# The opening of an encoder block: low weight parts behind the row statistics on GpSimd, rows five to seven taken together, one group's first sums later

## The chip, the cores and the metric

The kernel runs on one core of a Trainium2 chip. A core has five engines with queues of their own: TensorE (PE in the profile, with its weight loads as PEld), VectorE (DVE), ScalarE (ACT), GpSimd (POOL) and SyncE (SP, which here only issues transfers). Each works off its instructions in the order of the program; between engines they wait for one another by semaphores. The metric is the device time of one execution in microseconds (us).

## The reference

One transformer-like layer over 1024 tokens of width 1024, in float32. A layer norm of the input feeds one large projection with 11776 columns; dilated attention, a bidirectional gated recurrence, a merge, two more layer norms and a SwiGLU follow.

```python
h = layer_norm(x, ln_in_g, ln_in_b)
for l in range(DEPTH):                       # DEPTH = 1
    proj = h @ w_in[l]                       # (1024 x 1024) @ (1024 x 11776)
    aq, ak, av, hq, hf_fwd, hf_bwd, hi, hg, ga, gh = jnp.split(proj, split_idx, axis=-1)
    att = dilated_attention(aq, ak, av, slopes)
    rec = hgrn2(hq, hf_fwd, hf_bwd, hi, hg, lower_bounds[:, l], hgrn_norm_g[l])
    merged = jax.nn.sigmoid(ga) * (att @ w_att_up[l]) + jax.nn.sigmoid(gh) * (rec @ w_hgrn_up[l])
    h = layer_norm(DEEPNORM_ALPHA * h + merged @ w_o[l], ln1_g[l], ln1_b[l])
    gate, up = jnp.split(h @ w_ffn_in[l], 2, axis=-1)
    h = layer_norm(DEEPNORM_ALPHA * h + (jax.nn.silu(gate) * up) @ w_ffn_out[l], ln2_g[l], ln2_b[l])
```

Only the first layer norm and the first columns of `h @ w_in` are touched by the change.

## The kernel before

**Numbers in two parts.** TensorE multiplies in a rounded float32 format. A float32 operand is split into a high part (a rounding copy) and a low part (the difference), and each product is three matmuls: high by high (line 272), high by low (line 273) and low by high (line 274). For a weight block of 128x512 the high part is a cast on ScalarE (`w_hi`, line 214) and the low part a subtraction on GpSimd (`w_lo`, line 224), both in `split`. For the activations the high part is written by ScalarE (line 326) and the low part by VectorE (lines 401 and 402).

**The large product.** `h @ w_in` goes by a seven-product scheme over 2x2 blocks of 512. For each set of columns the products are numbered 1, 2, 6, 5, 7, 3, 4. Product 1 takes weight block `a11` with the activation form `b11`, product 2 `a12` with `b21`, product 6 the sum `s2` with `t2`, product 5 `s1` with `t1`, product 7 `s3` with `t3`, product 3 `s4` with `b22`, product 4 `a22` with `t4`. `stream` issues them in a list: first product 1 of two column sets for two groups each (places 0 to 3), then product 2 of the same four (places 4 to 7), then product 6 of the first set (places 8 and 9, one for each group), and so on. `prep(i)` splits the weights of place i; `sums(i)` makes `s1` (line 694, VectorE), `s2` (line 695, VectorE) and `s3` (line 696, GpSimd) for a product 6.

**The opening.** `phase0` makes the activation forms while `stream` already runs. The tokens come as eight row tiles of 128x1024, called row 0 to row 7 here. For each row `stats(tt)` gives mean and variance (two `bn_stats` on VectorE, line 343, an aggregate, line 345) and then three tiny GpSimd instructions (lines 346 to 348: add epsilon, power of minus one half, the shift); `norm(tt, q)` scales half q of the row on ScalarE (line 326) or VectorE (line 353); `turn` transposes it into PSUM on TensorE (line 362). Rows 0 to 3 give `b11` (half 0) and `b21` (half 1), rows 4 to 7 give the other column half of both, from which `t1`, `t2`, `b22`, `t3` and `t4` are made by subtractions (line 391 and others). The pool of row tiles has seven buffers, so row 7 is loaded only when row 0 has been transposed.

**What sets the order.** The kernel is recorded under a scheduler that reorders each engine's instructions by its own estimates of time. `ordered` and `behind` add an order without a semaphore: while `strict` is true, ScalarE's and VectorE's instructions of the opening stand in the order written; afterwards the scheduler may interleave them. `behind(ins, last)` puts one instruction behind another. `self.later` holds calls of `sums` for places 8 and 9 back until `phase0` has reached a given point.

Of the kernel before, what the change touches and what calls it, by code (L numbers as in the profile page):

```python
# [14 lines left out]
OP = mybir.AluOpType  # L15
# [64 lines left out]
class Block:  # L80
# [115 lines left out]
    def stats(self, pool, y, tag):  # L196

        nc = self.nc
        st = self.tiny.tile([128, 2, 6], F32, name=f"bn{tag}", tag="bnst", bufs=3)
        for j in range(2):  # L200
            nc.vector.bn_stats(st[:, j, :], y[:, HALF * j:HALF * (j + 1)])
        mv = self.tiny.tile([128, 4], F32, name=f"mv{tag}", tag="bnmv", bufs=3)
        self.rstd(mv, st)
        return mv
# [103 lines left out]
    def phase0(self, pool, work):  # L308


        nc, xs, banks = self.nc, [], {}
# [6 lines left out]
        w21 = [self.half("v21") for _ in range(4)]  # L318

        strict = True  # L320
        WARM = (11, 7, 6, 4)
        self.turned_last = None
        nbin = self.spare[:, 0:4]
# [5 lines left out]
        def dve(ins):  # L329
            return self.ordered("xdve", ins) if strict else ins  # L330
# [9 lines left out]
        def stats(tt):  # L340
            st = self.tiny.tile([128, 2, 6], F32, name="bn0", tag="bnst", bufs=3)
            for j in range(2):
                dve(nc.vector.bn_stats(st[:, j, :], xs[tt][:, HALF * j:HALF * (j + 1)]))
            mv = self.mv0[:, tt, :]
            dve(nc.vector.bn_aggr(mv[:, 0:2], st))
            nc.gpsimd.tensor_scalar(mv[:, 2:3], mv[:, 1:2], LN_EPS, None, op0=OP.add)
            nc.gpsimd.tensor_tensor(mv[:, 2:3], mv[:, 2:3], self.mhalf[:, 0:1], OP.pow)
            nc.gpsimd.tensor_scalar(mv[:, 3:4], mv[:, 0:1], mv[:, 2:3], -1.0, op0=OP.mult, op1=OP.mult)

        def norm(tt, q):  # L350
            x, mv = xs[tt][:, HALF * q:HALF * (q + 1)], self.mv0[:, tt, :]
            if tt > 5 and q == 0 or 0 < tt < 4 and q:
                return dve(nc.vector.tensor_scalar(x, x, mv[:, 2:3], mv[:, 3:4], op0=OP.mult, op1=OP.add))
            return act(x, x, AF.Identity, bias=mv[:, 3:4], scale=mv[:, 2:3])
# [49 lines left out]
        def run(n=1):  # L404
            for _ in range(n):
                next(work)
# [13 lines left out]
        for tt in range(4):  # L420
            n = norm(tt, 0)
            if 0 < tt < 3:
                self.gates[tt - 1] = n.ins.name
            run_up(WARM[tt])
            turn(tt, 0)
# [17 lines left out]
        lo("b11", 2, w11, bias[0][2])  # L443
        h = hi("b11", 3, w11, bias[0][3])
        lo("b11", 3, w11, bias[0][3])
        stats(4)
        self.gates += [h.ins.name] * 2
        run(2)
        load()
# [6 lines left out]
            self.left(lo("b21", k, w21, bias[1][k]))  # L456
        self.rest()
        strict = False
        for tt in range(5, 8):
            stats(tt)  # L460
        for q in range(2):
            for tt in range(4, 8):
                norm(tt, q)
# [2 lines left out]
        for k in (0, 2):  # L466
            for tt in range(4, 8):
                turn(tt, 0, (k, k + 1))
            for i in (k, k + 1):
                scaled(w12, i, 0, True)  # L470
                self.left(less(t1, i, 0, w11))
            if k == 0:
                for z in self.later:
                    z()
                self.later = None
            run()
        self.forms("b22")
        for k in (0, 2):
            for tt in range(4, 8):
                turn(tt, 1, (k, k + 1))  # L480
            for i in (k, k + 1):
                less(z2, i, 1, t1)
            parts = []
            for i in (k, k + 1):
                h = hi("t2", i, z2, bias[1][i]), lo("t2", i, z2, bias[1][i])
                parts.append(h)
            for i in (k, k + 1):
                ins = less(w12, i, 1, w12)
                if i > k:
                    self.behind(ins, parts[0][1].ins.name)  # L490
                g, b, z = column("gin", 4 + i), bias[1][i], self.xb["b22"][0][:, i, :]
                self.behind(act(z, banks[i], AF.Identity, bias=b, scale=g), h[0].ins.name)
                act(hb[i], z.bitcast(F32), AF.Identity, bias=nbin[:, i:i + 1])
                dve(nc.vector.scalar_tensor_tensor(self.xb["b22"][1][:, i, :], banks[i], g, hb[i], op0=OP.mult,
                                                   op1=OP.subtract))
            run()
# [157 lines left out]
    def stream(self, tiles, pool):  # L654


        nc, tc = self.nc, self.tc
        self.cols = [c for c, _ in tiles]
        O = self.ORDER
        order = [(n, (p,)) for p in O[:2] for n in (0, 1)]  # L660
        order += [(n, O[2:] if n < 2 else O) for n in range(len(tiles) // 4)]
        seq = [(n, g, p) for n, part in order for p in part for g in range(2)]
        after = {6: "a11", 7: "a21", 3: "a12", 4: "a22"}
        A, first = [{}, {}], {}
        for g in range(2):
            A[g]["a11"] = self.block(0, g, "a11")
        yield
        for g in range(2):
            first[g, 1] = self.block(1, g, "a11", pool)
        for g in range(2):  # L670
            A[g]["a12"] = self.block(0, g, "a12")
        yield
        for b in ("a21", "a22"):
            for g in range(2):
                A[g][b] = self.block(0, g, b)
        yield
        state = [[{}, {}], [{}, {}]]
        ready = {}

        def early(n):  # L680
            return tc.high_priority(offset=self.evac_ahead if n > 1 else 0)

        def sums(i, again=False):
            if i >= len(seq):
                return
            n, g, p = seq[i]
            a = A[g]
            if n == 0 and p == 6 and self.later is not None and not again:
                self.later.append(lambda: sums(i, True))
                return  # L690
            with early(n):
                if p == 6:
                    a["s1"] = self.blk.tile([128, 4, 128], F32, name="ws1", tag=f"s1{g}", bufs=1)
                    self.behind(nc.vector.tensor_add(a["s1"], a["a21"], a["a22"]))
                    self.left(nc.vector.tensor_sub(a["a11"], a["s1"], a["a11"]))  # L695
                    nc.gpsimd.tensor_sub(a["a21"], a["a22"], a["a11"])  # L696
                    a["s3"], a["s2"] = a["a21"], a["a11"]
                elif p == 3:
                    self.behind(nc.vector.tensor_sub(a["a12"], a["a12"], a["s2"]))
                    a["s4"] = a["a12"]  # L700

        def prep(i):
            if i >= len(seq):
                return
            n, g, p = seq[i]
            if n == 1 and p == 2:
                first[g, 2] = self.block(1, g, "a12", pool)
            with early(n):
                ready[i] = self.granules()
                self.split(*ready[i], first[g, p] if n == 1 and p < 3 else A[g][self.PRODUCTS[p][0]],  # L710
                           key="w" if i < 4 else None)
            if p in after and 4 * n + 4 < len(tiles):
                A[g][after[p]] = self.block(n + 1, g, after[p])

        def bank(n, g, p):
            if (n, p) in ((0, 5), (0, 2), (1, 2)):
                return self.ps_sd()
            return self.ps_pj(2 * g + (n + (p == 1)) % 2)

        def keep(ps, tag):  # L720
            t = self.ws.tile([128, HALF], F32, name="wkeep", tag=tag, bufs=1)
            nc.scalar.copy(t, ps)  # L722
            return t

        for i in range(3):
            prep(i)
        yield
        for i, (n, g, p) in enumerate(seq):
            late = i + 5 < len(seq) and seq[i + 5][0::2] == (1, 6)
            if not late:  # L730
                sums(i + 5)
            prep(i + 3)
            if late:
                sums(i + 5)
            s = state[n % 2][g]
            if p in (1, 2) or p == 5 and n < 2:
                s[min(p, 2)] = bank(n, g, p)
            ps = s[1 if p in (1, 6, 7, 4) else 2]
            hi, lo = ready.pop(i)
            xhi, xlo = self.xb[self.PRODUCTS[p][1]]  # L740
            for k in range(4):
                self.mm3(ps, hi[:, k, :], lo[:, k, :], xhi[:, k, :], xlo[:, k, :], p in (1, 2, 5) and k == 0, k == 3,
                         skip_group_check=True)
            self.leave(tiles[4 * n + 2 * g:4 * n + 2 * g + 2], p, ps, s, keep,
                       f"k{5 if (n, p) == (1, 1) else 1}{g}", f"k5{g}")
            yield 4 * n + 2 * g + 2 if p == 4 else 0
# [1291 lines left out]
```

## Time and profile before

| | |
|---|---|
| median of 3 runs | 2049.91 us (2048.36 to 2050.07) |
| the profiled execution | 2046.21 us |
| its span, first to last instruction | 2044.4 us |
| TensorE busy in the span | 2008.2 us (98%) |
| VectorE, ScalarE, GpSimd busy | 1315.3, 945.4, 1053.9 us |
| TensorE's mean granted clock | 0.998 |

In the views below a row of the timeline reads: start in us from the start of the span, duration in us, engine, source line, operation, output<-inputs, size, and in brackets the idle time of the engine before it with what ended it. A row of a table by windows gives the length of the window and, for each engine, the busy us and the number of instructions in it, then the granted clock (`PEclk`), the share of the transfer engines and GB/s.

### The profile page before, as it was taken

What the parts mean: (1) busy time and instruction counts of PE and PEld (TensorE: products, weight loads), DVE (VectorE), ACT (ScalarE), POOL (GpSimd) and SP (SyncE); (2) the same over time, 40 slices, a digit from 0 to 9 for tenths busy, and PEclk for the clock granted to TensorE, in tenths of its full rate; (3) what the DMA queues carried; (4) which work ended last, traced back from release to release, by engine and by line L of the source; (5) the groups of instructions that cost most, each with busy time, mean ns of one, the idle gap of its engine ahead of it and who ended that gap; (6) DMA issues with size and microseconds to landing.
All of it is one profiled execution on the core that took longest, in us unless ns stands there. A gap on an engine that the chain in (4) does not pass through costs nothing. (4 is left out here: it accounts for less than half of the span.)

```text
span 2044.4 us, 31027 instructions
## 1 busy us (share of the span) xinstructions
PE 2008.2 (98%) x11002; PEld 1667.9 (82%) x11002; DVE 1315.3 (64%) x2065; ACT 945.4 (46%) x1964; POOL 1053.9 (52%) x906
## 2 busy tenths in 40 slices
PE   7999999999999999999999999999999999999998
PEld 5788888788888888888888877887888888888886
DVE  7776545874458843778444236458776776767788
ACT  6553465544555535654365433244433333344541
POOL 5657644676447763467545652343766666630000
PEclk9999999999999999999999999999999999999999
DMA  5443533445333453343534478444444343358533
GB/s 159 142 140 125 174 114 104 133 136 172 118 123 126 141 163 104 124 139 124 169 99 149 132 246 258 121 142 127 154 139 139 128 146 129 121 168 293 165 95 127
DMA packets 274430, 296.92 MB, mean 145 GB/s; under 512 B 14114, under 2 KB 207459, under 8 KB 274275
## 3 DMA queue, kind: packets, MB, share of 16 engines
q1 hardware_dynamic: 267968, 273.73, 42.0%
q10 hardware_dynamic: 6306, 21.20, 2.8%
q8 instruction: 87, 1.43, 0.3%
q14 instruction: 69, 0.56, 0.1%
HBM read 200.77 MB, written 94.11 MB: 144 GB/s over the span
## 5 line engine op out<-in xcount | busy, mean ns | idle before, releaser
L224 POOL TENSOR_TENSOR w_lo<-wa,w_hi 128x512 fp32r<-128x512 f32 x272 | 365.3, 1351 | 266.1 <-ACT w_hi L214 223.7
L214 ACT CAST w_hi<-wa 128x512 fp32r<-128x512 f32 x272 | 169.2, 623 | 277.9 <-PE pj L273 163.3
L224 POOL TENSOR_TENSOR w_lo<-wsum,w_hi 128x512 fp32r<-128x512 f32 x88 | 129.1, 1477 | 109.9 <-PE sd L274 60.7
L224 POOL TENSOR_TENSOR w_lo<-f_raw,w_hi 128x512 fp32r<-128x512 f32 x66 | 100.7, 1534 | 52.2 <-ACT w_hi L214 51.0
L210 POOL TENSOR_TENSOR mv<-mv,mhalf 128x1 f32<-128x1 f32 x16 | 12.7, 791 | 221.7 <-DVE mv L209 221.6
L214 ACT CAST w_hi<-wsum 128x512 fp32r<-128x512 f32 x88 | 54.7, 622 | 115.5 <-PE sd L273 108.7
L272 PE MATMUL pj<-xt1hi,w_hi 128*128 128x512 f32 x252 | 99.9, 396 | 1.2 <-DVE evh L597 1.2
L214 ACT CAST gwsum<-a_raw 128x512 fp32r<-128x512 f32 (+1 forms) x78 | 48.2, 618 | 112.5 <-PE pj L273 56.0
L274 PE MATMUL pj<-xt1hi,w_lo 128*128 128x512 f32 x252 | 98.7, 392 | 0.9 <-POOL w_lo L224 0.9
L273 PE MATMUL pj<-xt1lo,w_hi 128*128 128x512 f32 x252 | 98.4, 391 | 0.0
L224 POOL TENSOR_TENSOR w_lo<-ws,w_hi 128x512 fp32r<-128x512 f32 x46 | 64.3, 1400 | 53.9 <-ACT w_hi L214 49.5
L581 DVE TENSOR_TENSOR evh<-wkeep,pj 128x512 f32<-128x512 f32 x45 | 30.9, 686 | 95.0 <-PE pj L274 55.0
L696 POOL TENSOR_TENSOR wa<-wa,wa 128x512 f32<-128x512 f32 x46 | 65.9, 1434 | 48.7 <-DVE wa L695 40.5
L570 DVE TENSOR_TENSOR evh<-wkeep,pj 128x512 f32<-128x512 f32 x66 | 58.1, 883 | 45.2 <-PE pj L274 37.9
L722 ACT COPY wkeep<-pj 128x512 f32<-128x512 f32 x136 | 79.5, 586 | 0.1
L273 PE MATMUL pj<-xt2lo,w_hi 128*128 128x512 f32 x192 | 75.5, 393 | 1.7 <-DVE xt2lo L402 1.7
L274 PE MATMUL pj<-xt2hi,w_lo 128*128 128x512 f32 x192 | 75.7, 394 | 1.3 <-POOL w_lo L224 1.3
L272 PE MATMUL pj<-xb11hi,w_hi 128*128 128x512 f32 x192 | 76.6, 402 | 0.0
L224 DVE TENSOR_TENSOR gwkeep<-a_raw,gwsum 128x512 fp32r<-128x512 f32 (+1 forms) x78 | 53.1, 681 | 36.3 <-ACT gwsum L214 33.5
L272 PE MATMUL pj<-xt4hi,w_hi 128*128 128x512 f32 x192 | 76.3, 397 | 0.0
L273 PE MATMUL pj<-xb11lo,w_hi 128*128 128x512 f32 x192 | 76.0, 397 | 0.0
L274 PE MATMUL pj<-xt4hi,w_lo 128*128 128x512 f32 x192 | 75.1, 391 | 0.7 <-POOL w_lo L224 0.7
(449 smaller groups left out, 6603.0 us busy)
## 6 DMA issues: line engine op xcount, KB each, us to landing
wa<-in_w_in_dram SPq DMA_DIRECT2D x184, 256.0 KB, 3.5
f_raw<-in_w_ffn_in_dram SPq DMA_DIRECT2D x44, 512.0 KB, 4.3
a_raw<-gd SPq DMA_DIRECT2D x30, 512.0 KB, 3.6
gd<-fc SPq DMA_DIRECT2D x44, 256.0 KB, 2.1
gd<-fs SPq DMA_DIRECT2D x33, 256.0 KB, 2.1
tg<-evh SPq DMA_DIRECT2D x32, 256.0 KB, 2.3
tg<-tg SPq DMA_DIRECT2D x16, 512.0 KB, 5.2
y<-ahs SPq DMA_DIRECT2D x16, 512.0 KB, 6.6
```

Source lines behind the costliest of these rows:

```text
L210: nc.gpsimd.tensor_tensor(mv[:, 2:3], mv[:, 2:3], self.mhalf[:, 0:1], OP.pow)
L214: ins = nc.scalar.copy(hi, src) if eng_hi == "act" else nc.vector.tensor_copy(hi, src)
L224: ins = e.tensor_sub(lo, src, hi.bitcast(F32))
L272: nc.tensor.matmul(ps, whi, xhi, start=first, stop=False, **kw)
L273: nc.tensor.matmul(ps, whi, xlo, start=False, stop=False, **kw)
L274: self.product = nc.tensor.matmul(ps, wlo, xhi, start=False, stop=last, **kw).ins.name
L570: self.left(nc.vector.tensor_tensor(o, self.order_src(add, g, kind), s, OP.add))
L581: self.left(nc.vector.tensor_add(t, add, ps))
L696: nc.gpsimd.tensor_sub(a["a21"], a["a22"], a["a11"])
L722: nc.scalar.copy(t, ps)
```

## The change

Four edits, all in the opening:

1. The low parts (GpSimd) of the weights at places 0 and 1 are put behind row 3's last statistics instruction, and those at places 4 and 5 behind row 6's.
2. The statistics of rows 4, 5 and 6 are written together at the point where only row 4's stood; row 7's stay where rows 5 to 7 stood.
3. `self.later` is set to an empty list, not to None, after its first use, so that the call of `sums` for place 9 (the second group's first product 6) is held back once more.
4. That held call is made behind the first two parts of `t2`.

```diff
@@ phase0
         strict = True
+        self.lo_after = {}
...
-            nc.gpsimd.tensor_scalar(mv[:, 3:4], mv[:, 0:1], mv[:, 2:3], -1.0, op0=OP.mult, op1=OP.mult)
+            ins = nc.gpsimd.tensor_scalar(mv[:, 3:4], mv[:, 0:1], mv[:, 2:3], -1.0, op0=OP.mult, op1=OP.mult)
+            if tt in (3, 6):
+                for i in (0, 1) if tt == 3 else (4, 5):
+                    self.lo_after[i] = ins.ins.name
...
         lo("b11", 3, w11, bias[0][3])
-        stats(4)
+        for tt in (4, 5, 6):
+            stats(tt)
...
         strict = False
-        for tt in range(5, 8):
-            stats(tt)
+        stats(7)
...
                 for z in self.later:
                     z()
-                self.later = None
+                self.later = []
...
                 h = hi("t2", i, z2, bias[1][i]), lo("t2", i, z2, bias[1][i])
                 parts.append(h)
+            if k == 0:
+                for z in self.later:
+                    z()
+                self.later = None
@@ stream, prep
-                self.split(*ready[i], first[g, p] if n == 1 and p < 3 else A[g][self.PRODUCTS[p][0]],
-                           key="w" if i < 4 else None)
+                lo = self.split(*ready[i], first[g, p] if n == 1 and p < 3 else A[g][self.PRODUCTS[p][0]],
+                                key="w" if i < 4 else None)
+                if i in self.lo_after:
+                    self.behind(lo, self.lo_after[i])
```

The scheduler turns this into a new order in the first 130 us; behind that each engine's order is the one before. In the changed program the lines of the helpers stand a little lower: the row statistics at 344 to 349, `norm` on VectorE at 357, the activations' low parts at 406, the subtractions at 395, the sums at 702 and 703.

GpSimd, row 3's statistics and the first low parts, before (`mv` is the statistics, `wa_260` and `wa_262` are the weights at places 0 and 1):

```order
L346 TENSOR_SCALAR mv_203<-mv_203 128x1
L347 TENSOR_TENSOR mv_203<-mv_203,mhalf 128x1
L224 TENSOR_TENSOR w_lo<-wa_260,w_hi 128x512
L348 TENSOR_SCALAR mv_203<-mv_203 128x1
L224 TENSOR_TENSOR w_lo<-wa_262,w_hi 128x512
```

and now:

```order
L347 TENSOR_SCALAR mv_203<-mv_203 128x1
L348 TENSOR_TENSOR mv_203<-mv_203,mhalf 128x1
L349 TENSOR_SCALAR mv_203<-mv_203 128x1
L224 TENSOR_TENSOR w_lo<-wa_260,w_hi 128x512
L224 TENSOR_TENSOR w_lo<-wa_262,w_hi 128x512
```

Row 3's last instruction moved ahead of the first low part.

GpSimd again, around row 7's three instructions, before (`wfirst` are the weights at places 6 and 7; the two at line 348 in one row belong to rows 5 and 6):

```order
L224 TENSOR_TENSOR w_lo<-wfirst,w_hi 128x512
L348 TENSOR_SCALAR mv_203<-mv_203 128x1 x2
L346 TENSOR_SCALAR mv_203<-mv_203 128x1
L224 TENSOR_TENSOR w_lo<-wfirst,w_hi 128x512
L347 TENSOR_TENSOR mv_203<-mv_203,mhalf 128x1
L348 TENSOR_SCALAR mv_203<-mv_203 128x1
```

and now (the first row belongs to row 6; `wa_272` and `wa_274` are places 4 and 5):

```order
L349 TENSOR_SCALAR mv_203<-mv_203 128x1
L224 TENSOR_TENSOR w_lo<-wa_272,w_hi 128x512
L224 TENSOR_TENSOR w_lo<-wa_274,w_hi 128x512
L347 TENSOR_SCALAR mv_203<-mv_203 128x1
L348 TENSOR_TENSOR mv_203<-mv_203,mhalf 128x1
L224 TENSOR_TENSOR w_lo<-wfirst,w_hi 128x512
L349 TENSOR_SCALAR mv_203<-mv_203 128x1
L224 TENSOR_TENSOR w_lo<-wfirst,w_hi 128x512
```

Rows 4 to 6 are done ahead of the low parts of places 4 and 5; row 7's last instruction comes behind three low parts, where it came behind all four.

VectorE, from the statistics of rows 4 to 7 (`bn_479` is row 7) to the low parts of `b21`, before:

```order
L343 BN_STATS bn_391<-xt 128x6 x2
L343 BN_STATS bn_465<-xt 128x6 x2
L343 BN_STATS bn_472<-xt 128x6 x2
L345 BN_AGGR mv_203<-bn_391 128x2
L387 TENSOR_SCALAR v_243<-sd,vc 128x512
L387 TENSOR_SCALAR v_245<-sd,vc 128x512
L345 BN_AGGR mv_203<-bn_465 128x2
L402 SCALAR_TENSOR_TENSOR xb21lo<-v_242,vc,xb21hi 128x512
L345 BN_AGGR mv_203<-bn_472 128x2
L343 BN_STATS bn_479<-xt 128x6 x2
L402 SCALAR_TENSOR_TENSOR xb21lo<-v_243,vc,xb21hi 128x512
```

and now, from row 6 on:

```order
L344 BN_STATS bn_405<-xt 128x6 x2
L344 BN_STATS bn_479<-xt 128x6 x2
L346 BN_AGGR mv_203<-bn_405 128x2
L391 TENSOR_SCALAR v_243<-sd,vc 128x512
L391 TENSOR_SCALAR v_245<-sd,vc 128x512
L346 BN_AGGR mv_203<-bn_479 128x2
L357 TENSOR_SCALAR xt<-xt,mv_203 128x512
L406 SCALAR_TENSOR_TENSOR xb21lo<-v_242,vc,xb21hi 128x512
L406 SCALAR_TENSOR_TENSOR xb21lo<-v_243,vc,xb21hi 128x512
L357 TENSOR_SCALAR xt<-xt,mv_203 128x512
L406 SCALAR_TENSOR_TENSOR xb21lo<-v_244,vc,xb21hi 128x512
L406 SCALAR_TENSOR_TENSOR xb21lo<-v_245,vc,xb21hi 128x512
```

Row 7's statistics moved ahead of the scaling and the low parts of `b21`, and the scaling of rows 6 and 7 (the two rows at line 357) moved in among those low parts.

VectorE, around the first low parts of `t2`, before (`wa_262` and `ws_571` belong to the second group):

```order
L694 TENSOR_TENSOR ws_571<-wa_280,wa_284 128x512
L595 TENSOR_TENSOR sd<-wkeep,sd 128x512
L391 SCALAR_TENSOR_TENSOR lent_xt4lo<-sd,vc,lent_xt3hi 128x512
L391 SCALAR_TENSOR_TENSOR lent_xt4hi<-sd,vc,lent_xt4hi 128x512
L391 SCALAR_TENSOR_TENSOR lent_xt4lo<-sd,vc,lent_xt3hi 128x512
L695 TENSOR_TENSOR wa_262<-ws_571,wa_262 128x512
L597 SCALAR_TENSOR_TENSOR evh<-evh,sd 128x512
L402 SCALAR_TENSOR_TENSOR xt2lo<-lent_xt4lo,vc,xt2hi 128x512
```

and now:

```order
L605 SCALAR_TENSOR_TENSOR evh<-evh,sd 128x512
L702 TENSOR_TENSOR ws_650<-wa_280,wa_284 128x512
L406 SCALAR_TENSOR_TENSOR xt2lo<-lent_xt4lo,vc,xt2hi 128x512
L395 SCALAR_TENSOR_TENSOR lent_xt4hi<-sd,vc,lent_xt4hi 128x512
L603 TENSOR_TENSOR sd<-wkeep,sd 128x512
L406 SCALAR_TENSOR_TENSOR xt2lo<-lent_xt4lo,vc,xt2hi 128x512
L703 TENSOR_TENSOR wa_262<-ws_650,wa_262 128x512
```

The second group's `s1` stands just ahead of the first low part of `t2` and its `s2` behind the second.

## The prediction

> **What bounds the kernel now.** I read the page, then TensorE's waits in the first 70 us, then the timeline of that stretch engine by engine. The page:
>
> ```profile
> span 2044.4 us, 31027 instructions
> PE 2008.2 (98%) x11002; PEld 1667.9 (82%) x11002; DVE 1315.3 (64%) x2065; ACT 945.4 (46%) x1964; POOL 1053.9 (52%) x906
> ```
>
> TensorE is idle for 2044.4 - 2008.2 = 36.2 us, so whatever it does not wait for is time won, and an instruction that others wait for in vain costs its wait and no more. The waits up to 70 us:
>
> ```profile
> PE sd L183 <- DMA vrows<-in_ln_in_b_dram: 5.2, 1, 5.2
> PE sd L362 <- ACT xt L326: 3.2, 3, 1.7
> PE pj L273 <- DVE xt2lo L402: 1.7, 2, 1.0
> PE sd L272 <- DVE lent_xt3hi L391: 1.5, 1, 1.5
> ```
>
> The first, 5.2, is the start and is not touched. The change works on the rest: 3.2 on scaled rows, 1.7 on `t2`'s low parts, 1.5 on the first subtraction. There is one more loss, in the clock (length, busy us of PE, PEld, DVE, ACT, POOL, then the granted clock):
>
> ```profile
> 10.23:13.65 3.42, 2.71 (x21) 1.99 (x19) 1.79 (x5) 2.38 (x4) 3.07 (x6) 1.00 0.98 351
> 13.65:17.06 3.41, 1.63 (x13) 1.39 (x14) 2.94 (x4) 2.49 (x4) 1.56 (x3) 1.00 1.17 306
> 17.06:20.47 3.41, 3.41 (x13) 2.74 (x12) 2.88 (x5) 3.38 (x7) 0.53 (x1) 0.50 1.12 332
> 37.54:40.95 3.41, 1.92 (x9) 1.51 (x9) 2.64 (x5) 2.47 (x5) 0.00 (x0) 1.00 0.21 77
> ```
>
> After a window in which TensorE was busy for 1.63 of 3.41 us the next ran at 0.50; after one with 1.92 it did not.
>
> **Part 1: low parts behind row 3's statistics.** Rows of the opening, in order of time:
>
> ```profile
> 10.32 0.56 POOL L347 TENSOR_TENSOR mv<-mv,mhalf 128x1 f32<-128x1 f32 x1
> 10.98 0.27 POOL L348 TENSOR_SCALAR mv<-mv 128x1 f32<-128x1 f32 x1
> 11.10 0.95 DVE L353 TENSOR_SCALAR xt<-xt,mv 128x512 f32<-128x512 f32 x2
> 11.76 0.72 POOL L347 TENSOR_TENSOR mv<-mv,mhalf 128x1 f32<-128x1 f32 x1
> 12.45 1.27 POOL L224 TENSOR_TENSOR w_lo<-wa,w_hi 128x512 fp32r<-128x512 f32 x1
> 13.81 0.27 POOL L348 TENSOR_SCALAR mv<-mv 128x1 f32<-128x1 f32 x1
> 14.12 0.81 ACT L326 ACTIVATE xt<-xt,mv 128x512 f32<-128x512 f32 x1 [1.51 <-POOL mv L348]
> 14.12 1.47 DVE L353 TENSOR_SCALAR xt<-xt,mv 128x512 f32<-128x512 f32 x1 [2.06 <-POOL mv L348]
> 19.11 0.63 PE L274 MATMUL pj<-xb11hi,w_lo 128*128 128x512 f32 x1
> ```
>
> For the row before, line 348 starts 0.10 after line 347's end (10.88 to 10.98). In the new order row 3's starts at 12.48 + 0.10 = 12.58 instead of 13.81: **1.2 us earlier** for the scaling, the transposes, `b11` and the first product. The two low parts then end near 12.85 + 2 x 1.27 = 15.4; the first reader (line 274) stands at 19.11, so they stay hidden. What they touch is VectorE's line 353: it took 1.47 beside a low part, and 0.95 for two alone. It ran beside one before and will again, so nothing is added.
>
> The Trainium skill, page "GPSIMD Engine Reference", section "Key points", says that GpSimd shares its SBUF interfaces with VectorE and contends with VectorE instructions in a two-port mode or with two SBUF inputs. The 1.47 agrees. By that rule every line 353 and line 402 beside a low part would be stretched so, which would put the sum of part 2 at its late end.
>
> With TensorE starting 1.2 us earlier, the window from 13.65 holds 1.63 + 1.2 = 2.8 busy us, more than the 2.71 that kept the clock. The half clock from 17.06 goes away: between 0 (if `b11`'s low parts pace TensorE anyway) and 3.41 x 0.5 = 1.7 us; I take 1.5, since TensorE was busy for all 3.41. The first group of products, which ended at 30.62, then ends near 30.62 - 1.2 - 1.5 = 27.9.
>
> **Part 2: rows 4 to 7.** What this gain meets:
>
> ```profile
> 20.10 3.65 DVE L343 BATCH_NORM_STATS2 bn<-xt 128x6 f32<-128x512 f32 x6
> 21.20 0.34 SPq L251 DMA_DIRECT2D xt<-in_x_dram  x1
> 23.78 1.35 DVE L387 TENSOR_SCALAR v<-sd,vc 128x512 f32<-128x512 f32 x2
> 25.16 0.70 DVE L402 SCALAR_TENSOR_TENSOR xb21lo<-v,vc,xb21hi 128x512 fp32r<-128x512 f32 x1
> 25.90 1.27 DVE L343 BATCH_NORM_STATS2 bn<-xt 128x6 f32<-128x512 f32 x2
> 30.23 0.39 PE L274 MATMUL pj<-xb11hi,w_lo 128*128 128x512 f32 x1
> 31.82 0.44 PE L362 MATMUL sd<-tabs_sb,xt 128*128 128x128 f32 x2 [1.21 <-ACT xt L326]
> ```
>
> and the transfers, by windows (the last two numbers are their share and GB/s):
>
> ```profile
> 24.00:25.00 1.00, 1.00 (x6) 0.82 (x5) 1.00 (x2) 0.01 (x1) 0.00 (x0) 1.00 1.03 339
> 26.00:27.00 1.00, 1.00 (x6) 0.84 (x5) 1.00 (x2) 1.00 (x4) 1.00 (x1) 1.00 0.10 24
> ```
>
> The wait of 1.21 for row 4's scaling goes, since rows 4 to 6 have their statistics early. But VectorE's queue now has row 7's `bn_stats` ahead of `b21`'s scaling and low parts. Row 7's load waits for row 0's transposes and was issued at 21.20; transfers ran at 339 GB/s until about 26. Two or three us earlier it queues behind the weight blocks, so I let it land at about 24.4 (bounds: 23.5, if the transfers have no gap, and 25.9, where its statistics start now). VectorE is free at about 20.10 - 1.2 + 3.65 + 0.3 = 22.9 and stands still for 1.5. Then 1.27 of statistics, 1.35 of scaling, an aggregate (0.2) and row 6's line 353 (0.5 to 1.5) give the first low part of `b21` at 28.0 to 29.5, where it came at 25.16. TensorE, ready at 27.9, has 7 transposes first and waits 0 to 1 us.
>
> The larger new wait is row 7's line 353, which stands between the second and third low part of `b21`. It needs row 7's GpSimd rows:
>
> ```profile
> 33.80 0.23 POOL L346 TENSOR_SCALAR mv<-mv 128x1 f32<-128x1 f32 x1
> 33.99 1.46 POOL L224 TENSOR_TENSOR w_lo<-wfirst,w_hi 128x512 fp32r<-128x512 f32 x1
> 35.19 0.69 DVE L581 TENSOR_TENSOR evh<-wkeep,sd 128x512 f32<-128x512 f32 x1 [0.88 <-PE sd L274]
> 35.41 0.56 POOL L347 TENSOR_TENSOR mv<-mv,mhalf 128x1 f32<-128x1 f32 x1
> 36.06 0.27 POOL L348 TENSOR_SCALAR mv<-mv 128x1 f32<-128x1 f32 x1
> 38.31 1.41 DVE L391 SCALAR_TENSOR_TENSOR lent_xt3hi<-sd,vc,lent_xb22hi 128x512 f32<-128x512 f32 x2 [1.40 <-ACT lent_xt4hi L326]
> ```
>
> Row 6 is aggregated at 24.4 + 1.27 + 0.2 = 25.9; its three GpSimd rows take 0.2 + 0.6 + 0.3, to 27.0. Two low parts (2 x 1.3) end at 29.6, row 7's first two rows (0.8) at 30.4, a third low part (1.3) at 31.7, line 348 at 32.0; stretched by VectorE's neighbours, at 32.8. So row 7 is scaled at 32.0 to 33.4 (0.55 to 1.5 long) and the last two low parts (1.4) end at 34.0 to 36.0. TensorE waits 1 to 3 us inside its first `b21` product, which ends about 0.7 us behind its last low part, at 34.7 to 36.7 (before: the wait at line 581 ended at 35.19). Line 581 (0.6) and line 391 follow at 35.3 to 37.3, against 38.31 before: 1.0 to 3.0 earlier. I take **1.6**, nearer the late end, because VectorE's line 353 and 402 run beside low parts there, as the 1.47 did. So of the 2.7 + 1.2 won by then more than half is given back.
>
> **Part 3: the second group's sums.** Around `t2`'s first low parts stands now:
>
> ```profile
> 45.33 0.68 DVE L695 TENSOR_TENSOR wa<-ws,wa 128x512 f32<-128x512 f32 x1
> 46.09 1.28 POOL L696 TENSOR_TENSOR wa<-wa,wa 128x512 f32<-128x512 f32 x1 [0.84 <-DVE wa L695]
> 46.53 1.39 DVE L402 SCALAR_TENSOR_TENSOR xt2lo<-lent_xt4lo,vc,xt2hi 128x512 fp32r<-128x512 f32 x1
> 47.42 1.65 POOL L224 TENSOR_TENSOR w_lo<-wa,w_hi 128x512 fp32r<-128x512 f32 x1
> 49.10 1.76 DVE L402 SCALAR_TENSOR_TENSOR xt2lo<-lent_xt4lo,vc,xt2hi 128x512 fp32r<-128x512 f32 x1
> 49.26 0.40 PE L274 MATMUL pj<-xt2hi,w_lo 128*128 128x512 f32 x1
> ```
>
> Taking line 695 (0.60 from start to start) from ahead of `t2`'s first low part, and GpSimd's work from beside both (1.39 and 1.76 against the 0.70 of line 402 at 25.16), brings `t2` forward by 0.6 to 2.3 in its place; TensorE waited 1.7 for it. In return the second group's `s2` comes behind the second low part: at 49.10 - 0.60 - 0.69 + 0.70 = 48.5, 3.2 later than 45.33, then line 696 and the low part (1.28 + 1.3) end near 51.8, against 49.07. Its reader stood at 49.26; three matmuls and four transposes (1.1 us) moved ahead of it, so 1.5 us of new wait stand against up to 1.7 of old. Between -1.0 and +1.5; I take +0.7, because TensorE now waits first for `w_hi` and then for `w_lo` of the same weights.
>
> From 58 on the shuffled rows (line 401 ahead of line 699, a swap of two loads) meet no wait of 1.5 or more (the list of waits above goes to 70), so I let them cost 0.3, with 0 and 0.8, half of such a wait, as ends.
>
> **The sum.** 1.6 earlier at 38, less 0.7, less 0.3: 0.6 us shorter. Against the profiled execution that is 2046.21 - 0.6; the runs' median lies 3.7 above that execution, and I take the 0.6 off the median: 2049.91 - 0.6 = **2049.3**. Adding the ends of parts 2 and 3, the likeliest case alone reaches from -3.0 - 1.0 to -1.0 + 1.5 + 0.8, so 2045.9 to 2051.2. A difference of 0.2% (4.1 us) is about what a measurement of this kernel can tell from no change.
>
> **The rivals.** *All of it is kept.* Row 7's part of GpSimd is not late, its wait hides behind TensorE's transposes, and the 1.2 + 1.5 + 1.2 reach the end together with 0.6 of part 3: 4.5 us, 2045.4. For it speaks that TensorE has ten transposes to fill with; against it that VectorE cannot pass row 7's load and three low parts, by the durations above. It needs line 348 of row 7 by about 30. Chance 0.10.
>
> *The clock gate falls behind row 4.* If TensorE is busy for less than about 1.7 us of a window, the next runs at half clock and costs up to 1.7. Waits for `b21` (28 to 35) and for `t2` (45 to 51) could do this three times: 5.1 - 0.6 = 4.5 us slower, 2054.4. The row with 1.92 shows how near it is now; against three such windows speaks that part 1 removes one and that the waits found are 1 to 3 us each. It decides from 1.7 us idle in one window on. Chance 0.10.
>
> The Trainium skill, page "TensorE: Matmul & The Clock Gate", section "What's actually happening", has the gate close only after an idle window of about 3.4 us; the trace, with half a window busy, disagrees, and by the page alone neither the gain of 1.5 nor this rival would exist.
>
> *Moved, not won.* The new wait for row 7 takes everything, and the sums cost 1.5: up to 2.5 us slower, 2051. The late ends of part 2 give it. Chance 0.20.
>
> **The numbers.** 0.60 for the likeliest, 0.20 for moved but not won, 0.10 each for the others. The first two stay within 4.1 us: same 0.80, faster 0.10, slower 0.10. The range leaves the far half of the outer cases out: 2045.8 to 2052.6.
>
> **What would show it.** In the new trace: row 3's scaling near 12.9; no window at 0.50 behind it; VectorE idle before row 7's `bn_stats`; a wait of 1 to 3 us inside the first `b21` product; line 391 starting near 36.7; `t2`'s low parts near 0.7 each. I am wrong if row 7 lands before 23 or TensorE gets a half-clock window between 30 and 52.

## The result, and the profile after

The changed kernel is slower: 2052.45 us against 2049.47 us, medians of 15 runs each. The ratio is 1.0018 with a 95% interval of 1.0010 to 1.0026, some 3.7 us (2.1 to 5.3). The prediction had 2049.3, 0.6 us shorter than before: a wrong sign, and a loss just under the 0.2% that was called "same". The profiled execution's span is 2053.1 us, 8.7 above the one before; a good part of that is what differs between any two executions (below), so the experiments go by the timed runs.

TensorE's waits up to 70 us in the changed kernel, the six longest:

```profile
PE sd L183 <- DMA vrows<-in_ln_in_b_dram: 5.4, 1, 5.4
PE sd L366 <- DVE xt L357: 1.9, 2, 1.3
PE pj L273 <- DVE xt2lo L406: 1.3, 2, 0.9
PE sd L366 <- DVE v L391: 1.0, 1, 1.0
PE sd L366 <- ACT xt L327: 1.0, 2, 0.7
PE sd L273 <- DVE xb21lo L406: 0.9, 1, 0.9
```

But for the first, the start, no single wait is longer than 1.3, where the kernel before had one of 1.7. The table by windows of 3.41 us (length, busy us of PE, PEld, DVE, ACT, POOL, then the granted clock, the transfers' share and GB/s), cut at the edges of this execution's clock, shows where the time went:

```profile
25.10:28.52 3.42, 3.24 (x15) 2.39 (x13) 1.26 (x3) 3.42 (x6) 0.00 (x0) 1.00 0.20 53
28.52:31.93 3.41, 1.52 (x9) 1.05 (x9) 3.41 (x7) 3.41 (x7) 3.00 (x5) 1.00 0.01 2
31.93:35.34 3.41, 2.52 (x8) 1.76 (x7) 1.90 (x2) 1.36 (x3) 3.24 (x4) 0.50 0.00 0
35.34:38.76 3.42, 2.14 (x7) 1.17 (x7) 2.80 (x3) 1.64 (x3) 1.64 (x3) 0.50 0.00 0
38.76:42.17 3.41, 2.63 (x10) 1.71 (x8) 1.55 (x3) 1.65 (x3) 0.00 (x0) 0.50 0.00 0
42.17:45.58 3.41, 3.41 (x10) 2.74 (x9) 2.98 (x5) 1.31 (x2) 1.01 (x1) 0.50 0.21 77
45.58:49.00 3.42, 3.42 (x20) 2.90 (x20) 2.23 (x4) 1.32 (x2) 1.52 (x2) 1.00 0.00 0
52.41:55.82 3.41, 1.62 (x5) 0.75 (x5) 3.41 (x7) 3.21 (x6) 1.92 (x2) 1.00 0.01 2
55.82:59.24 3.42, 3.42 (x11) 2.83 (x12) 3.42 (x5) 0.35 (x1) 1.82 (x2) 0.50 0.21 77
```

The half clock behind row 3 is gone, as forecast (the kernel before had it from 17.06 to 20.47). In its place the clock falls to 0.50 at 31.93, after a window that was busy for 1.52 us, and stays there for four windows; a fifth follows at 55.82. VectorE's timeline (start, duration, and in brackets the idle time before it) shows what made the window of 1.52:

```profile
22.16 1.23 DVE L344 BATCH_NORM_STATS2 bn<-xt 128x6 f32<-128x512 f32 x2
27.26 1.29 DVE L344 BATCH_NORM_STATS2 bn<-xt 128x6 f32<-128x512 f32 x2 [3.87 <-DMA xt<-in_x_dram]
28.57 1.36 DVE L391 TENSOR_SCALAR v<-sd,vc 128x512 f32<-128x512 f32 x2
31.41 2.42 DVE L406 SCALAR_TENSOR_TENSOR xb21lo<-v,vc,xb21hi 128x512 fp32r<-128x512 f32 x2
35.89 1.47 DVE L357 TENSOR_SCALAR xt<-xt,mv 128x512 f32<-128x512 f32 x1 [2.07 <-POOL mv L349]
41.23 1.41 DVE L395 SCALAR_TENSOR_TENSOR lent_xt3hi<-sd,vc,lent_xb22hi 128x512 f32<-128x512 f32 x2
```

VectorE stands still for 3.87 us for row 7's load, with `b21`'s scaling queued behind. The load had been issued early, at 18.96 by SP's queue, but it needed until 27.26:

```profile
15.93 2.92 SPq L251 DMA_DIRECT2D wa<-in_w_in_dram  x4
18.96 1.81 SPq L251 DMA_DIRECT2D xt<-in_x_dram  x1
```

Four weight blocks of 256 KB (`a21` and `a22`) stand just ahead of it. Before, the same load was issued at 21.20 and had landed by 25.90 at the latest. In the second profile of the changed kernel (below) it landed at 25.62, so 27.26 is not its fixed value.

### The profile page after: what moved, and what is told of

Read it like the earlier page. It is cut to its first block, busy times and chain, and to the rows that moved or that the text cites. A ratio compares the mean times of both kernels' runs of the same rounds, so it can differ in the third digit from the quotient of the medians.

```text
span 2053.1 us, 31033 instructions
## 1 busy us (share of the span) xinstructions
PE 2013.8 (98%) x11002; PEld 1671.2 (81%) x11002; DVE 1319.4 (64%) x2065; ACT 944.5 (46%) x1964; POOL 1050.5 (51%) x906
## 3 DMA queue, kind: packets, MB, share of 16 engines
q10 hardware_dynamic: 6306, 21.20, 2.7%
## 5 line engine op out<-in xcount | busy, mean ns | idle before, releaser
L272 PE MATMUL pj<-xt2hi,w_hi 128*128 128x512 f32 x192 | 76.5, 399 | 0.9 <-ACT w_hi L214 0.5
L224 DVE TENSOR_TENSOR gwkeep<-a_raw,gwsum 128x512 fp32r<-128x512 f32 (+1 forms) x78 | 53.1, 681 | 36.3 <-ACT gwsum L214 33.4
```

Source lines behind the costliest of these rows:

```text
L224: ins = e.tensor_sub(lo, src, hi.bitcast(F32))
L272: nc.tensor.matmul(ps, whi, xhi, start=first, stop=False, **kw)
```

## The experiments

Times are the ratio's to the kernel before on the same chip, in us of its 2049.5, with the 95% interval. "Part A" is the first half of edit 1 (places 0 and 1 behind row 3), "B" edit 2, "C" the second half of edit 1 (places 4 and 5 behind row 6), "D" edits 3 and 4. All of them leave each engine's order behind 130 us as it was.

### Part A alone

```diff
-            if tt in (3, 6):
-                for i in (0, 1) if tt == 3 else (4, 5):
+            if tt == 3:
+                for i in (0, 1):
```

(and without edits 2, 3 and 4).

> The kernel before with the first half of edit 1 alone: the low parts of places 0 and 1 behind row 3's last statistics. Only the order of three instructions of GpSimd differs. If part 1 of the prediction holds, row 3 is scaled 1.2 us earlier (12.9 instead of 14.1), the window behind it is not at half clock, the first group of products ends 1.2 to 2.7 us earlier (28 to 29.4 instead of 30.6), and of that about 2 us reaches the end: 2 us faster than before (1 to 2.7). Rival: row 7's load, which lands at about 26 whatever TensorE does, takes the gain back at once: within 0.5 us of before.

Measured: 0.9982 (0.9972 to 0.9992), 3.7 us faster (1.6 to 5.7). Its windows:

```profile
13.64:17.06 3.42, 2.60 (x19) 2.23 (x20) 3.42 (x5) 2.93 (x6) 2.11 (x2) 1.00 1.12 305
17.06:20.47 3.41, 3.41 (x19) 2.80 (x18) 2.88 (x6) 3.41 (x7) 1.50 (x2) 1.00 1.10 330
```

The window that had been busy for 1.63 is now busy for 2.60, and no half clock follows. The rival falls: the gain stays. Part 1 of the prediction was right, and its 2.7 lies inside the interval.

### Part D alone, and the change without it

```diff
-            if tt in (3, 6):
+            if tt in ():
```

(edits 3 and 4 kept, edit 2 undone), and the other way round:

```diff
-                self.later = []
+                self.later = None
...
-            if k == 0:
-                for z in self.later:
-                    z()
-                self.later = None
```

> The kernel before with edits 3 and 4 alone: the second group's sums behind the first two parts of t2. The prediction's part 3 gave 0.7 us slower (between 1.0 faster and 1.5 slower). The new theory, from the trace of the changed kernel, where the window from 52.4 to 55.8 was busy for 1.62 of 3.41 us and the next was at 0.50: the waits for the second group's weights come to about half a window and cost a half-clock window of 1.7 beside themselves, 2 to 3 us slower than before. Rival: the waits for t2 and those for the weights cancel, within 0.5 us.

> The changed kernel without edits 3 and 4 (edits 1 and 2 remain). If the late row 7 and the half clock from 31.9 to 45.6 carry the loss, they stay, and the time is 1 to 2 us less than that of the changed kernel, still 1 to 2.5 us above before. If the sums carry it (the rival), the time is 0 to 3 us below before. In its trace VectorE should still stand idle for 2 us or more ahead of row 7's statistics, and TensorE's clock should be at 0.50 for one window or more between 30 and 46.

D alone: 1.0015 (1.0006 to 1.0025), 3.1 us slower (1.2 to 5.1). Without D: 1.0001 (0.9990 to 1.0013), 0.2 us above before (2.0 below to 2.7 above), which is 3.5 under the changed kernel and a little under what was expected. Its trace has the expected signs, VectorE idle for 3.12 us ahead of row 7's statistics (at 26.98) and two windows at half clock:

```profile
34.14:37.56 3.42, 0.89 (x5) 0.33 (x4) 1.95 (x2) 0.87 (x2) 2.56 (x3) 1.00 0.00 0
37.56:40.97 3.41, 2.62 (x7) 1.51 (x5) 1.48 (x4) 1.78 (x3) 0.00 (x0) 0.50 0.00 0
40.97:44.38 3.41, 3.30 (x10) 2.81 (x11) 3.41 (x7) 1.46 (x3) 0.10 (x1) 0.50 0.21 77
```

So D carries nearly the whole difference to before (3.5, uncertain by about 3 us either way, as the difference of two measurements), and A's gain is what B and C eat up.

### Part C out as well

```diff
-            if tt in (3, 6):
-                for i in (0, 1) if tt == 3 else (4, 5):
+            if tt == 3:
+                for i in (0, 1):
```

(on the kernel without D: parts A and B remain).

> The changed kernel without edits 3 and 4 and without the second half of edit 1: the low parts of places 4 and 5 are free again to stand ahead of row 6's statistics, row 3's part and the statistics of rows 4 to 6 in one go remain. Against the kernel without edits 3 and 4 alone (2050.6 beside 2049.8 for before) it prices the hold on places 4 and 5: three low parts at 1.3 us that stood between row 6 and row 7's last statistics are out of the way, so row 7 is scaled 1 to 3 us earlier: 1 to 4 us below that kernel, 1 to 4 us below before. Rival (row 7's load decides alone): the same as that kernel, within 1 us.

Measured: 0.9991 (0.9982 to 1.0001), 1.8 us faster (3.7 faster to 0.2 slower), 2.0 under the kernel with C. Row 7's statistics start at 25.33 here. B beside A costs 3.7 - 1.8 = 1.9, C another 2.0. Each is a difference of two measurements with intervals of some 2 us either way, so neither is clear of zero by itself. Their signs agree with the traces: with C two half-clock windows between 37 and 45, without it none from 10 to 870.

### The late load

The weight blocks `a21` and `a22` are requested one product later, so that row 7's load stands ahead of them:

```diff
-        for b in ("a21", "a22"):
-            for g in range(2):
-                A[g][b] = self.block(0, g, b)
         yield
...
         for i, (n, g, p) in enumerate(seq):
+            if i == 1:
+                for b in ("a21", "a22"):
+                    for z in range(2):
+                        A[z][b] = self.block(0, z, b)
```

On the changed kernel, on the kernel with A and B, and as a control on the kernel before:

> The changed kernel with one thing more: the loads of the weight blocks a21 and a22 (four of 256 KB), which stand ahead of row 7's load in the queue, are issued behind it. They are read first by line 702 at 42.6 us. If the late load (row 7's statistics started at 27.26, forecast 24.4) is the step that failed, they now start at 25 or earlier, VectorE's idle time before them falls from 3.87 to 1.5 or less, row 7 is scaled 2 us or more earlier, and the time is 2 to 3 us below that of the changed kernel. If GpSimd's queue or the half clock alone decides (rival), row 7's statistics come earlier and the time stays within 0.7 us of the changed kernel.

> The kernel with row 3's part and the statistics of rows 4 to 6 in one go (without the hold on places 4 and 5 and without edits 3 and 4), and with the loads of a21 and a22 behind row 7's load. If the late load and the queue of low parts on GpSimd are the two costs of the first three edits, neither is left: row 7's statistics start before 25, no window at half clock stands between 17 and 46, and the time is 4 to 6 us below before, 1 to 2 us below the kernel with row 3's part alone (2046.2). If row 3's part was all there was to win (rival): 3 to 4 us below before, the same as that kernel.

> The kernel before with the loads of a21 and a22 behind row 7's load, nothing else. It lands row 7 some 3 us earlier, as in the changed kernel with the same edit (6.8 us faster by it). If the load costs only because edit 2 put row 7's statistics ahead of b21's scaling and low parts, nothing waits for it here, and the time is that of before, within 1 us. If the late load costs by itself, in every order (rival), it is 2 us or more below before.

On the changed kernel: 0.9985 (0.9974 to 0.9997), 3.1 us faster than before and 6.8 under the changed kernel, more than the 2 to 3 expected. VectorE and SP's queue there:

```profile
18.19 0.34 SPq L251 DMA_DIRECT2D xt<-in_x_dram  x1
21.52 2.42 DVE L344 BATCH_NORM_STATS2 bn<-xt 128x6 f32<-128x512 f32 x4
23.96 1.35 DVE L391 TENSOR_SCALAR v<-sd,vc 128x512 f32<-128x512 f32 x2
```

Row 6's and row 7's statistics (x4) run through without an idle gap, `b21`'s scaling starts at 23.96 instead of 28.57, row 7 is scaled at 31.26 instead of 35.89, and no window between 11 and 47.9 is at half clock. The edit takes away the whole wait for the load and not only the part that the forecast had missed, so the 6.8 is the price of the load in this order; no run has it land near the forecast's 24.4. With A and B alone the same edit gives 0.9976 (0.9967 to 0.9984), 4.9 us faster than before (3.3 to 6.8): the fastest of all, faster than both kernels compared here. From part A alone (3.7 faster) it can't be told apart. On the kernel before it gives 1.0002 (0.9993 to 1.0011): nothing. The load cost only in the orders where VectorE's queue has `b21`'s work behind row 7's statistics.

### Row 7's statistics behind the low parts of `b21`

```diff
         self.rest()
-        strict = False
         stats(7)
+        strict = False
```

> The changed kernel with row 7's statistics behind the four low parts of b21 in VectorE's queue; row 7's load is issued and lands as in the changed kernel (25 to 27.5). If it is the order (VectorE standing still for the load with b21's work queued behind) that costs, VectorE is not idle ahead of b21's scaling, no half clock stands between 30 and 40, and the time is 2 to 5 us below the changed kernel. If the late row 7 costs by its own scaling and transposes, wherever its statistics stand (rival), it is within 1 us of the changed kernel.

Measured: 1.0014 (1.0005 to 1.0023), 2.9 us slower than before and 0.6 under the changed kernel, which ran on the same chip (its second run, below). My expectation failed, and the rival holds. VectorE no longer stands still for the load, but row 7 is now scaled at 37.44 instead of 35.89, and its transposes hold up TensorE just the same:

```profile
35.34:38.76 3.42, 1.21 (x7) 0.73 (x7) 1.28 (x4) 1.80 (x3) 1.06 (x3) 1.00 0.21 79
38.76:42.17 3.41, 2.23 (x5) 1.82 (x6) 3.04 (x5) 2.07 (x4) 0.00 (x0) 0.50 0.00 0
42.17:45.58 3.41, 3.41 (x10) 2.56 (x9) 1.00 (x3) 0.62 (x1) 2.44 (x2) 0.50 0.00 0
```

It isn't the place in the queue alone. In the kernel before row 7 was scaled at 36.37 and line 391 started at 38.31; here the same subtraction starts at 39.13, so nothing of A's gain gets past row 7. Since row 7 is scaled later here than in the changed kernel, what VectorE's standing still costs by itself isn't priced by this run.

### The clock

Two kernels change how long TensorE is busy, and little else. In the changed kernel 26 transposes of the identity are put into its idle places (`fill`, into a slot that row 7's transposes overwrite); in the kernel before, ten more of those that already stand ahead of row 3's (`fill` itself, and the order that holds the rows' transposes behind it, are left out here):

```diff
+        FILL = (7, 5, 14)
...
+                if k == 0 and tt < 7:
+                    fill(FILL[tt - 4])
```

```diff
-        WARM = (11, 7, 6, 4)
+        WARM = (11, 7, 6, 14)
```

> The changed kernel with 26 extra transposes of the identity on TensorE (7 behind row 4's first two transposes, 5 behind row 5's, 14 behind row 6's), at the places where TensorE stands still between 28.3 and 33.2; what they write is overwritten by row 7's transposes. They remove no wait: VectorE's, GpSimd's and the loads' work is the same. If the half clock comes from windows in which TensorE is busy for less than about half (1.52 of 3.41 us ahead of the half clock at 31.9), the window at half clock begins at least one window (3.4 us) later or not at all, fewer than 13.7 us are at half clock between 30 and 46, and the time is 1.5 to 4 us below the changed kernel. If the waits alone decide (rival), or if only a wholly idle window would close the clock, it is 0 to 1 us above the changed kernel.

> The kernel before with ten more transposes of the identity ahead of row 3's (14 in place of 4), where TensorE stands idle for 1.74 us; they take 10 x 0.11 = 1.1 us. No wait is removed. Half-window rule: the window that was busy for 1.63 of 3.41 us is now busy for 2.7, the half clock from 17.07 to 20.47 is gone, the first group of products ends up to 1.7 us earlier, and the time is 0.5 to 1.7 us below before. Rival (the clock follows something else than TensorE's busy share): the half clock stays, and the time is that of before.

With the transposes the changed kernel takes 1.0002 (0.9989 to 1.0014), 0.4 us above before and 3.3 under the changed kernel (uncertain by about 3 us either way), though 26 instructions were added. VectorE's order is the changed kernel's up to 40.6; behind that the scheduler moved a few instructions of VectorE, ScalarE and SP as well, so not all of the 3.3 need be the clock's. Its windows:

```profile
29.93:33.35 3.42, 3.42 (x25) 2.76 (x23) 1.83 (x2) 3.04 (x6) 3.25 (x4) 1.00 0.00 0
33.35:36.76 3.41, 1.28 (x6) 0.87 (x7) 2.92 (x4) 1.84 (x3) 1.58 (x3) 1.00 0.00 0
36.76:40.18 3.42, 3.42 (x11) 2.46 (x11) 2.76 (x5) 2.02 (x4) 0.00 (x0) 0.50 0.00 1
40.18:43.59 3.41, 3.41 (x20) 2.89 (x19) 2.78 (x5) 1.03 (x2) 2.35 (x2) 1.00 0.21 76
```

The half clock begins at 36.76 instead of 31.93, behind the next idle place, and lasts one window, since TensorE is then busy without a gap. The waits alone can't explain a half clock that moves when TensorE is kept busy. The page "TensorE: Matmul & The Clock Gate" of the Trainium skill, section "What's actually happening", has the clock close after an idle window of about 3.4 us; none of these was idle, and the measurement decides.

The other kernel, in which TensorE's order alone differs, gained nothing: 1.0005 (0.9996 to 1.0014), 1.0 us above before, and my expectation failed. In its profile the half clock at 17 is gone, as expected, but one stands at 38, where the profile of the kernel before had none:

```profile
13.64:17.06 3.42, 2.97 (x24) 2.73 (x23) 2.56 (x3) 1.97 (x3) 1.69 (x3) 1.00 1.16 307
17.06:20.47 3.41, 3.41 (x23) 2.97 (x22) 2.88 (x5) 3.38 (x7) 0.01 (x1) 1.00 1.12 329
34.76:38.18 3.42, 1.54 (x11) 0.83 (x8) 1.56 (x3) 2.81 (x6) 0.74 (x2) 1.00 0.10 37
38.18:41.59 3.41, 3.21 (x8) 2.56 (x9) 3.41 (x7) 1.09 (x2) 0.00 (x1) 0.50 0.11 40
```

TensorE's timeline ahead of row 3:

```profile
13.79 1.94 PE L373 MATMUL sd<-tabs_sb 128*128 128x128 f32 x14
15.57 0.60 PE L362 MATMUL sd<-tabs_sb,xt 128*128 128x128 f32 x4
```

Row 3's transposes start at 15.57, where they started at 14.98 before: the fourteen transposes take 1.94 us, and behind them no idle time is left, so row 3 waits for them now. What the clock gave at 17, the filler and the later half clock took. How much of each the timed runs hold isn't settled, so no timed run here prices a half-clock window by itself.

### The changed kernel again, and D where there is room

> The changed kernel once more, for a second profile beside the others on one chip. If the late load and the half clock behind it are its rule and not one execution's accident, row 7's statistics start at 25 to 27.5 with VectorE idle for 2 us or more ahead of them, at least one window stands at half clock between 30 and 46, and the time is 2 to 5 us above before. If the half clock was an accident of the one profile (rival), none stands there and the clock is full from 21 to 80.

> The kernel with row 3's part, the statistics of rows 4 to 6 in one go and a21 and a22 behind row 7's load (2045.3 beside 2049.4 for before), with edits 3 and 4 added, the second group's sums behind the first parts of t2. On the kernel before they cost 3.1 us, on the kernel with edits 1 and 2 3.5. If that cost is theirs alone, by the new waits for the second group's weights near 50, they cost 1 to 3.5 us here too: 2046.5 to 2049. If it came of TensorE being near half-busy windows already (rival), they cost less than 1 us here, where no window at half clock stands before 80.

The changed kernel again: 1.0017 (1.0007 to 1.0027). In this second execution row 7's statistics start at 25.62, after 2.43 us of idle time, and the half clock is there again, with two windows instead of four, and once more behind `t2`:

```profile
29.09:32.50 3.41, 1.71 (x10) 1.15 (x9) 3.11 (x3) 3.41 (x6) 3.24 (x4) 1.00 0.01 2
32.50:35.91 3.41, 1.40 (x5) 0.59 (x4) 1.64 (x2) 1.41 (x3) 2.86 (x4) 0.50 0.00 0
35.91:39.33 3.42, 3.04 (x8) 1.87 (x8) 1.49 (x3) 1.84 (x3) 0.00 (x0) 0.50 0.00 0
49.57:52.98 3.41, 2.03 (x8) 1.09 (x8) 3.41 (x6) 2.80 (x6) 2.33 (x2) 1.00 0.01 2
52.98:56.39 3.41, 3.41 (x11) 2.72 (x10) 3.30 (x5) 0.73 (x2) 1.43 (x2) 0.50 0.21 77
```

D on the fastest kernel: 0.9988 (0.9977 to 0.9998), 2.5 us faster than before, so D costs 2.4 there. The changed kernel with the same loads, 3.1 faster, is this one with C added: once row 7 lands early, C costs nothing that these runs can tell. The profile with D has the same mark:

```profile
43.64:47.05 3.41, 1.52 (x6) 0.65 (x5) 3.41 (x7) 3.30 (x6) 1.83 (x2) 1.00 0.01 2
47.05:50.46 3.41, 3.41 (x10) 2.87 (x11) 3.41 (x6) 0.25 (x1) 1.92 (x2) 0.50 0.21 77
```

Of the seven profiles with D, six have exactly one window at half clock that begins between 47 and 56 (the seventh is the one with row 7's statistics moved back); of the seven without D, that of the kernel before among them, none has one there. D's share was measured three times, at 3.1, 3.5 and 2.4; the last is uncertain by about 3 us either way. The window itself is 3.41 x 0.5 = 1.7. Where edit 2 is in, waits give a part of the rest. In the changed kernel without D, TensorE's wait for `t2`'s low parts is

```profile
PE pj L273 <- DVE xt2lo L406: 0.3, 1, 0.3
```

and it is 0.3 in the two other kernels with edit 2 and without D as well. With D it is 1.3, and 0.5 for `w_hi` comes new. On the kernel before, D lowers that wait, from 1.7 to 1.2, so there most of what lies beyond the window isn't located. D also reorders TensorE, VectorE and the transfers between 75 and 105 us; the profile of D alone has two more half-clock windows there, at 86 and 103, but of the six other profiles with D only one has any there (at 99), so what the rest is stays open.

## Why the prediction was wrong

**Part 1, row 3 earlier and no half clock behind it: right.** The first group's last product was forecast to end near 27.9; in the changed kernel it starts at 27.83 and ends at 28.23, against 30.62 before. By itself the part is worth 3.7 us (1.6 to 5.7) at the end, where the sum had 2.7 at 28. But the place of the half clock was one execution's: the kernel before with row 7's load ahead and the one with D alone have TensorE's order of before up to 42, and in their profiles the clock is not halved at 17 but once at 39.47 and once at 38.38. Part A alone has no window at half clock from 10 to 2030.

**Part 2: the step that failed is "I let it land at about 24.4 (bounds: 23.5 ... and 25.9)".** Row 7's load landed at 27.26 in one profile, beyond the late bound, and at 25.62 in the other, just inside it: 2.9 and 1.2 later than the sum had it. I saw that it would be issued 2 to 3 us earlier and would queue behind the weight blocks, and then took a landing time from the stretch before, 1.5 us ahead of the old one. Issued earlier, it met a queue with 1 MB just ahead, and came no earlier to speak of; with that 1 MB behind it, it was there before VectorE asked. The early bound's condition, transfers without a gap, was met (never under 275 GB/s from 15 to 25 in either profile), and still it came after 25: before, one gap had stood there (114 GB/s from 22 to 23), so an earlier issue had little to win. Everything that followed moved along: the first low part of `b21` came at 31.41 (forecast 28.0 to 29.5), row 7 was scaled at 35.89 (32.0 to 33.4), line 395 started at 41.23 (36.7), 2.9 us later than before instead of 1.6 earlier. One addition was off besides: statistics, scaling, aggregate and line 353 behind 24.4 end at 27.7 to 28.7 and not at 28.0 to 29.5. The mechanism, VectorE's queue behind row 7's load and row 7 behind three low parts on GpSimd, was right; parts B and C, which make it, cost about 1.9 and 2.0, where the sum had 1.1 for both together (2.7 won at 28, 1.6 left at 38).

**The clock: a rival at 0.10, and it happened.** "The clock gate falls behind row 4" was priced at three windows of 1.7. I had read the row with 1.63 rightly as the cause of a half clock, and I had put the limit near 1.7. What I did not see is that the half clock does not end by itself after one window: 2.52, 2.14 and 2.63 busy us at half clock left it closed, only 3.41 opened it. A wait inside a half-clock window can keep the next one at half clock too, and with the late row 7 there were such waits up to 42. In the kernel before the one half-clock window had been full (3.41), so its trace showed the end after one window and not the condition.

**Part 3: mis-sized.** The sums were put at +0.7 (between -1.0 and +1.5), with 0.3 for the rows shuffled behind them, and cost 2.4 to 3.5. What was forecast for `t2` came true beside the kernel before: its first two low parts took 0.75 each instead of 1.39 and 1.76, and the wait for them fell from 1.7 to 1.3. But with edit 2 and without D they took 0.74 each already and the wait was 0.3, so the gain that the sum credited to the sums was no longer there to be had. And the wait for `w_hi` (0.5) and for `t2`'s high part (0.4) fell into the same window, which then held 1.62 busy us, and the half clock that I had left to the rival followed.

**The parts together.** Taken apart one after the other, B and C cost 2.8 us more than the sum had, D (3.5 on this kernel, against 0.7 + 0.3) 2.5 more, and A won 1.0 more: 4.3, the way from 0.6 faster to 3.7 slower.

**The numbers.** Same was given 0.80 with a bound of 4.1 us, and the change cost 3.7. The range reached to 2052.6 and the median is 2052.45, which is luck, since the sign was the other: "moved, not won" (up to 2.5 slower, 0.20; that is 2052.4, where 2051 was written) and the clock rival (4.5 slower, 0.10) together are what happened, and I treated them as alternatives though the same wait feeds both.

## What to carry to other kernels

An instruction that is moved ahead in an engine's queue takes its input's landing time with it: ask what stands ahead of that load in the transfer queue, since the load that was issued earlier here, behind the same bytes, landed no earlier to speak of. Count waits of an engine with a clock gate by window, not one by one: several of under 1 us that meet in one window can cost a half-clock window beside themselves, and more if further waits keep the clock closed. A gain and its loss are best tried apart: here the first half of edit 1 won as much as the whole change lost.

## What the runs showed of the hardware that was not expected

- **The clock reopens only after a nearly full window.** In the 14 profiles, from 15 to 2000 us, nine half-clock windows were followed by another at 0.50; they hold 1.40 to 2.74 busy us of 3.41 (2.52, 2.14 and 2.63 in the changed kernel). All 38 that were followed by full clock hold 3.00 or more. If the busy time counted by the clock, the limit for opening would lie between 2.74 x 0.5 = 1.37 and 3.00 x 0.5 = 1.50, below every limit that fits the closing (next point), so one limit of half a window for both doesn't come out of these rows.
- **The limit for closing isn't sharp in the profile's busy time.** At full clock every window with less than 1.59 busy us closed it and none with more than 2.03 did. Between them both occur: 1.62, 1.63, 1.71 and 2.03 closed it; 1.92 (before, 37.54) and 1.69 (the kernel before with row 7's load ahead, 29.23) did not.
- **The windows lie differently in each execution.** All last 3.41 us, but they start at different points of the program: the clock fell at 31.93 and 32.50 in the two profiles of the changed kernel, and at 17.06, 38.38 and 39.47 in three profiles with TensorE's order of before up to there. So the same order of instructions meets different windows, which fits the spread of the runs of one kernel (2043.58 to 2052.45 before); it was not separated from other causes.
- **One profile records a clock of 0.95 throughout.** In that of part D alone the granted clock stands at 0.95 from 14.5 us on, but for its half-clock windows (mean 0.945). The matmuls did not go at that pace: line 272 on `xt1hi` took 397 ns there and 396 before, and the span, 2055.3, is 0.5% longer than the 2044.4 before. What the record stands for is open.
